# A hybrid attention block on one Trainium2 core: another order for the preparation of the NSA operands, for the modulation strips and for the first stage's weight rounding

## The chip, the core and the metric

The kernel runs on one core of one Trainium2 chip. The metric is device microseconds of a whole launch; lower is better. A core has five engines that run side by side, each through its own list of instructions strictly in order: PE (TensorE, matrix products and transposes; its weight loads are listed apart as PEld), DVE (VectorE), ACT (ScalarE), POOL (GpSimd) and SP (SyncE, which here only issues DMA transfers). An instruction that has to wait for another engine or for a transfer holds up all that stand behind it on its own engine.

## The reference

One transformer block, 512 tokens by 1024 channels, in float32:

```
mod = silu(c) @ ada_w + ada_b                      # six vectors of 1024: sh1, sc1, gt1, sh2, sc2, gt2
h   = rms_norm(x, norm1_gain) * (1 + sc1) + sh1
z   = h @ w_in                                     # 1024 x 4408, cut into latents, q_n, k_c, v_c, k_s, ...
y_mla = mla_attention(latents of z) @ w_o_mla
y_nsa = nsa_attention(q_n, k_c, v_c, k_s, v_s, k_w, v_w, gate logits of z) @ w_o_nsa
x   = x + gt1 * ((sigmoid(g1) * y_mla + sigmoid(g2) * y_nsa) @ w_out)
h2  = rms_norm(x, norm2_gain) * (1 + sc2) + sh2
x   = x + gt2 * ((silu(h2 @ w_gate) * (h2 @ w_up)) @ w_down)
```

In `nsa_attention`, `k_c` and `v_c` (128 columns of z each) are first compressed: overlapping blocks of 32 tokens, plus a position table, go through `silu(flat @ w1) @ w2` with w1 of 2048 x 256. q is normed per head, rotated and used against the compressed, the selected and the windowed keys; the three results are mixed with `sigmoid(gate logits)`.

## The kernel before, in words

Every large product is made in float32 precision from three products of rounded parts. A weight chunk is loaded into a tile `raw`, ACT rounds it into `whi`, DVE subtracts to get the rest `wlo`, and PE adds `hi*whi + hi*wlo + lo*whi` in PSUM. `raw`, `whi` and `wlo` have four buffers each, so that a fourth chunk ahead is the most that can be prepared.

The change lies in the first fifth of the program, up to the start of the NSA attention:

1. `first_gemm` makes `h` and the first 768 columns of `w_in` (query, k_c, v_c) together. For each of eight channel blocks k it needs the modulation column of that block: strips of `ada_w` (tiles `araw`) are multiplied by silu(c) and added up by DVE (`acc`), PE sums them over the partitions (`pm`), DVE makes `modc` from it, PE transposes x (`px`), ACT writes `hTh` (rounded) and `h`, DVE writes `hTl`. PE then runs three groups of eight matmuls per block: A (whi, hTh), B (wlo, hTh) and C (whi, hTl). The instructions of this stage carry a hand-written order per engine (`Paced.strict`). SP issues its transfers in a fixed order too, each waiting for the one eight places earlier.
2. `gemm_wide` for the next 536 columns (`segb2`: k_s, v_s, k_w, v_w, gate logits; tiles `wa`, `wb`), with the preparation of the NSA operands woven in, a step at a time.
3. Three `gemm_tok` passes of 352 columns (`sega`, tiles `ga`; 96 matmuls each), with the rest of the preparation woven in.

The preparation is a chain of generators: `compress_blocks` (transposes of `ZC` to `X2`, position table added in `FF`, rounded and split into `FS`), `compress_w1` (32 matmuls `ph` per K or V, with w1 chunks as weights), `compress_w2` (`hid`, silu, `po`), `compress_out` (norm and rotation of the compressed keys on DVE, `kcr` and `kcd`), `prep_q` (square and sum on ACT and DVE, norm; gain and rotation on POOL; transpose `pq`; split into `QS`), `prep_k` (the same for `UK`, `kd`, `pk`, `KH`, `KL`) and `prep_gates` (exponential on ACT). Beside it `mods()` loads further strips of `ada_w` for the later modulation vectors into the single tile `strip`; DVE multiplies each in two instructions into `macc`, and the next strip can only be issued when both are done.

All calls go through one recording helper, so nearly every instruction carries line 152; rows are told apart by their tiles. After the hand-ordered stage a scheduler places the instructions on each engine; what it made of both programs is shown with the change.

Of the kernel before, what the change touches and what calls it, by code (L numbers as in the profile page):

```python
# [20 lines left out]
P = 128  # L21
S = 512
# [93 lines left out]
def hybrid_block(ctx, tc, a, out):  # L116
# [366 lines left out]
    def first_gemm(w, c0, na, nb, consume_a, consume_b):  # L483
# [57 lines left out]
        products(1, "A")  # L541
        add_rows(acc, s23, 2, (1, 2))
        lo_of(hT[1][1], h, hT[1][0])
        add_rows(acc, s23, 2, range(3, KD))
        products(1, "B")
        scale_x(2 * P, 4 * P, ())
        products(1, "C")
        px = turn_x(2)
        for k in range(2, KD, 2):
            pm = tp.tile([P, S], F32, name="pm", tag="tp")  # L550
            high(k)
            low(k)
            mod_sum(pm, 2, [(acc, ones)], True, True)
            if k > 2:
                products(k - 1, "C")
            more = k + 2 < KD
            if more:
                sn = strips(k + 2, 2)
                load(k + 2)
                load(k + 3)  # L560
            mod_done(pm, k, 2)
            h = modulate(k, px)
            products(k, "A")
            high(k + 1)
            low(k + 1)
            px = turn_x(k + 1)
            lo_of(hT[k][1], h, hT[k][0])
            products(k, "B")
            if more:
                acc = add_rows(None, sn, 2, range(2))  # L570
            h = modulate(k + 1, px)
            if k == 2:
                scale_x(4 * P, D, ())
            products(k, "C")
            if more:
                add_rows(acc, sn, 2, (2, 3))
            lo_of(hT[k + 1][1], h, hT[k + 1][0])
            products(k + 1, "A")
            products(k + 1, "B")
            if more:  # L580
                add_rows(acc, sn, 2, range(4, KD))
                px = turn_x(k + 2)
            else:
                products(k + 1, "C")
        h_last[:] = dve.last, act.last
# [190 lines left out]
        rsqrt(rsf, msf, cpp, f"n{nm}")  # L776
        yield rs

    def prep_q():
        for _ in norm_rows(UQ, 8, "q", rs_n):  # L780
            yield
        for t in range(NT):
            u = UQ[t]
            pool.tensor_tensor(out=u, in0=u, in1=g_n[:, 0:1, :].broadcast_to([P, 8, 64]), op=ALU.mult)
            rope(pool, u[:, :, 0:16], *tables(t, FULL, 8), cpp, f"nq{t}")
            yield
            pq = tp.tile([P, 4, P], F32, name=f"pq{t}", tag="tp")
            for j in range(4):
                pe.transpose(pq[:, j, :], u[:, 2 * j : 2 * j + 2, :].rearrange("p a b -> p (a b)"), ident)
            tcol = slice(t * P, (t + 1) * P)  # L790
            for par in range(2):
                top = slice(64 * par, 64 * par + 64)
                bot = slice(64 * (1 - par), 64 * (1 - par) + 64)
                hi_of(QS[top, par::2, tcol], pq[top, :, :])
                lo_of(QS[bot, par::2, tcol], pq[top, :, :], QS[top, par::2, tcol])
            yield
# [20 lines left out]

    def prep_gates():
        ge = gn.rearrange("p t c -> p (t c)")
        act.activation(out=ge, in_=ge, func=AF.Exp, scale=-1.0)  # L820
        dve.tensor_scalar(out=ge, in0=ge, scalar1=1.0, scalar2=None, op0=ALU.add)
        dve.reciprocal(out=ge, in_=ge)
        gv = gn[:, 0, :].rearrange("p (h b) -> p h b", b=3)
        dve.tensor_scalar(out=gv[:, :, 0], in0=gv[:, :, 0], scalar1=kc_t[:, C_VALID : C_VALID + 1], scalar2=None, op0=ALU.mult)
        yield

    cmp_state = {}

    def compress_blocks(i, nm):
        X2 = cpp.tile([P, 2, 528], F32, name=f"X2_{i}", tag="X2", bufs=1)  # L830
# [22 lines left out]

    def compress_w1(i, nm):
        FS = cmp_state[i]
        ph = sc.tile([P, S], F32, name="ph", tag="sc") if i else mm.tile([P, S], F32, name="ph", tag="mm")
        cmp_state[i] = ph
        w1 = a[f"cmp_w1_{nm}"][0]
        for k0 in range(0, 16, 4):
            h, l = wchunk(rows(w1, k0 * P, 4, 0, 256), 4, 256)  # L860
            for j in range(4):
                pe.matmul(ph[:, :256], FS[:, k0 + j, :], h[:, j, :], start=(k0 + j == 0), stop=False)
                pe.matmul(ph[:, :256], FS[:, k0 + j, :], l[:, j, :], start=False, stop=(k0 + j == 15))
            yield

    def compress_w2(i, nm):
        ph = cmp_state[i]
        hd = cpp.tile([64, 256], F32, name=f"hid{i}", tag="hid", bufs=1)
        act.activation(out=hd, in_=ph[64:128, :256], func=AF.Copy)
        dve.tensor_tensor(out=hd, in0=hd, in1=ph[0:64, :256], op=ALU.add)  # L870
        act.activation(out=hd, in_=hd, func=AF.Silu)
        yield
        pt = tp.tile([P, S], F32, name="pt", tag="tp")
        for j in range(2):
            pe.transpose(pt[:, j * 64 : (j + 1) * 64], hd[:, j * P : (j + 1) * P], ident[:64, :64])
        hidT = cpp.tile([P, 2, 64], F32, name=f"hidT{i}", tag="hidT", bufs=1)
        dve.tensor_copy(out=hidT.rearrange("p a b -> p (a b)"), in_=pt[:, :128])
        w2 = cpp.tile([P, 2, 64], F32, name=f"w2{i}", tag="w2", bufs=1)
        sp.dma_start(out=w2, in_=a[f"cmp_w2_{nm}"][0].rearrange("(j p) d -> p j d", p=P))
        po = tp.tile([P, S], F32, name="po", tag="tp")  # L880
        for j in range(2):
            pe.matmul(po[:64, :64], hidT[:, j, :], w2[:, j, :], start=(j == 0), stop=(j == 1))
        yield
        cmp_state[i] = po
# [85 lines left out]
    def mods():  # L970
# [16 lines left out]
        def finish_row(acc, m, slot, hf):  # L987
            if hf == 0:
                gt[slot] = mcp.tile([P, D], F32, name=f"gt{slot}", tag="gt", bufs=1)
            o = gt[slot][:, hf * S : (hf + 1) * S]  # L990
            sp.dma_start(out=o, in_=a["ada_b"][:, m * D + hf * S : m * D + (hf + 1) * S].broadcast_to([P, S]))
            pm = tp.tile([P, S], F32, name="pm", tag="tp")
            pe.matmul(pm, ones, acc, start=True, stop=True)
            dve.tensor_tensor(out=o, in0=pm, in1=o, op=ALU.add)
# [29 lines left out]
    def need_mod(slot):  # L1024
        while (slot, 1) not in mods_done:
# [2 lines left out]
    mods_gen = mods()  # L1028
    mods_begun = []
    segb2 = gemm_wide(hA, w_in, KD, SEG_B + 768, 280, 256, use_w, use_s, pair_first=True)  # L1030
    pq, pk = prep_q(), prep_k()
    K, V = (0, "k"), (1, "v")
    prep = chain(compress_blocks(*K), part(pq, 5), compress_w1(*K), part(pq, 4), compress_w2(*K), compress_blocks(*V),
                 compress_out(*K), pq, compress_w1(*V), part(pk, 5), compress_w2(*V), pk, compress_out(*V), prep_gates())
    ep_st = scope()
    strip_src["pool"] = ep_st.enter_context(tc.tile_pool(name="ep", bufs=1, reuse_waits="tile"))

    def with_mods(main, every):
        for i, _ in enumerate(main):
            if i % every == 0:  # L1040
                later(mods_gen, 2 if mods_begun else 1)
                mods_begun.append(i)
            yield

    weave(with_mods(segb2, 3), prep, 1, 1)
    sega = chain(*[gemm_tok(hA, w_in, KD, SEG_A + c0, 352, use_a(c0), tag=f"a{c0}") for c0 in (0, 352, 704)])
    weave(with_mods(sega, 6), prep, 2, 1)
    run(prep)
    later(mods_gen, 1)
    ep_st.close()  # L1050
    strip_src.clear()
    cp_st.close()
# [807 lines left out]
```

## Time and profile before

| | |
|---|---|
| median of 3 runs | 875.28 us (873.97 to 875.67) |
| the profiled execution, its own time | 874.82 us |
| its span, from the first to the last instruction | 873.0 us |
| PE busy | 841.4 us (96%), 5052 matmuls |
| DVE busy | 668.7 us (77%) |
| ACT busy | 457.2 us (52%) |
| POOL busy | 119.2 us (14%) |
| mean granted PE clock | 0.989 |

In the rows a time is microseconds from the start of the span: start, duration, engine, operation, tile written <- tiles read, shapes; in square brackets the idle time of the engine just before and what ended it. Matmuls overlap in the pipeline, so their rate is read from start to start and not from the duration. Around the change, the first product stage runs from about 2 to 62 us, `segb2` from 62 to 88, `sega` from 100 to 158, and the attention follows.

### The profile page before, as it was taken

The numbers are of one execution on the slowest core, as the hardware profiler recorded it, in microseconds if no ns is written. First come the engines' busy times: TensorE is split into PE (matmuls) and PEld (weight loads), VectorE is DVE, ScalarE is ACT, GpSimd is POOL, SyncE is SP. The second block draws the span as 40 slices with busy tenths as digits, with TensorE's granted clock in tenths as the row PEclk, the third lists the DMA queues.
The fourth block names the chain that finished last, engine by engine and source line by source line (L and its number), as shares of the span: only waits on it lengthen the run. The fifth ranks groups of instructions, "written<-read, shape, count | busy, mean of one in ns | idle before, by whom it ended". The sixth has DMA issues, their size and how long they took to land.

```text
span 873.0 us, 13961 instructions
## 1 busy us (share of the span) xinstructions
PE 841.4 (96%) x5052; PEld 740.4 (85%) x5052; DVE 668.7 (77%) x1392; ACT 457.2 (52%) x962; POOL 119.2 (14%) x203
## 2 busy tenths in 40 slices
PE   8899799899999999899999999999999999999997
PEld 8789689777777789787788889898999889988996
DVE  5778896668888568688879877975887858965875
ACT  4643655678666567665634255551456326641550
POOL 0002516525342012212200000000000000000000
PEclk9999799999999999999999999999999999999999
DMA  9956646222201123325597753452233313343312
GB/s 309 326 166 189 197 143 170 74 72 74 72 13 61 43 92 98 120 97 180 172 321 253 256 166 118 128 152 90 73 98 121 121 51 113 104 125 92 98 49 97
DMA packets 95706, 115.54 MB, mean 132 GB/s; under 512 B 6565, under 2 KB 68885, under 8 KB 95637
## 3 DMA queue, kind: packets, MB, share of 16 engines
q1 hardware_dynamic: 92596, 108.32, 40.4%
q10 hardware_dynamic: 2400, 4.23, 1.3%
q0 software_dynamic: 640, 2.10, 0.6%
q8 instruction: 40, 0.66, 0.3%
q14 instruction: 30, 0.24, 0.1%
HBM read 106.24 MB, written 8.39 MB: 131 GB/s over the span
## 4 chain that ended last, share of the span: by engine, by line
PE 79%; DVE 8%; DMA 7%; ACT 3%; issue 2%; SPq 1%; ACTq 0%; DVEq 0%
PE d L152 14%; PE fx L152 12%; PE gp L152 9%; PE fy L152 9%; PE pt L152 4%; DMA strip<-in_ada_w_dram 4%; PE av L152 3%; PE ga L152 3%; PE gwo L152 3%; PE gym L152 3%; PE fg L152 3%; PE yn L152 3%; PE wo L152 3%; PE gq L152 2%; PE fu L152 2%
## 5 line engine op out<-in xcount | busy, mean ns | idle before, releaser
L152 ACT ACTIVATE whi<-raw 128x1024 fp32r<-128x1024 f32 (+4 forms) x161 | 141.6, 897 | 133.1 <-PE d L152 51.6
L152 DVE TENSOR_TENSOR wlo<-raw,whi 128x1024 fp32r<-128x1024 f32 (+4 forms) x138 | 149.4, 1090 | 61.3 <-ACT whi L152 60.8
L152 PE MATMUL d<-whi,mh 128*128 128x512 f32 (+1 forms) x180 | 69.9, 391 | 0.6 <-DVE tm L152 0.5
L152 PE MATMUL d<-wlo,mh 128*128 128x512 f32 (+1 forms) x180 | 70.2, 390 | 0.0
L152 PE MATMUL d<-whi,ml 128*128 128x512 f32 (+1 forms) x180 | 67.6, 389 | 0.0
L152 ACT ACTIVATE s<-s,mn 128x384 f32<-128x384 f32 (+2 forms) x96 | 52.5, 548 | 23.1 <-DVE mn L152 22.5
L152 DVE TENSOR_TENSOR plo<-pt,phi 128x512 fp32r<-128x512 f32 (+2 forms) x78 | 46.3, 602 | 19.1 <-ACT phi L152 18.7
L152 PE MATMUL gp<-hTh,whi 128*128 128x512 f32 x128 | 54.4, 425 | 0.0
L152 ACT ACTIVATE phi<-pt 128x512 fp32r<-128x512 f32 (+2 forms) x78 | 39.9, 525 | 27.5 <-PE pt L152 26.9
L152 PE MATMUL gp<-hTh,wlo 128*128 128x512 f32 x128 | 51.2, 400 | 0.0
L152 PE MATMUL gp<-hTl,whi 128*128 128x512 f32 x128 | 50.7, 396 | 0.0
L152 ACT ACTIVATE whi<-s 128x1024 fp32r<-128x1024 f32 (+1 forms) x36 | 30.2, 846 | 32.0 <-PE d L152 18.0
L152 PEld LDWEIGHTS d<-whi,mh 128*128 128x128 f32 x180 | 33.7, 188 | 8.9 <-DVE tm L152 1.2
L152 PE MATMUL fx<-h2h,whi 128*128 128x256 f32 x144 | 41.1, 286 | 0.0
L152 PE MATMUL fx<-h2l,whi 128*128 128x256 f32 x144 | 40.8, 283 | 0.0
L152 PE MATMUL fx<-h2h,wlo 128*128 128x256 f32 x144 | 40.8, 283 | 0.0
L152 PEld LDWEIGHTS d<-whi,ml 128*128 128x128 f32 x180 | 33.8, 188 | 7.7
L152 PEld LDWEIGHTS d<-wlo,mh 128*128 128x128 f32 x180 | 33.8, 188 | 7.4
L152 DVE TENSOR_TENSOR wlo<-s,whi 128x1024 fp32r<-128x1024 f32 (+1 forms) x36 | 33.7, 951 | 7.4 <-ACT whi L152 7.4
L152 PE MATMUL pt<-ident,s 128*128 128x128 f32 x232 | 37.4, 278 | 0.1
L152 POOL TENSOR_TENSOR wlo<-raw,whi 128x512 fp32r<-128x512 f32 x24 | 31.7, 1341 | 23.1 <-ACT whi L152 23.1
L152 PEld LDWEIGHTS pt<-ident,s 128*128 128x128 f32 x232 | 28.1, 142 | 7.6 <-issue 2.1
(432 smaller groups left out, 2666.2 us busy)
## 6 DMA issues: line engine op xcount, KB each, us to landing
raw<-in_ffn_w_gate_dram SPq DMA_DIRECT2D x22, 512.0 KB, 3.9
raw<-in_ffn_w_up_dram SPq DMA_DIRECT2D x22, 512.0 KB, 4.1
raw<-in_ffn_w_down_dram SPq DMA_DIRECT2D x22, 512.0 KB, 3.9
raw<-in_ada_w_dram SPq DMA_DIRECT2D x18, 512.0 KB, 5.0
araw<-in_ada_w_dram SPq DMA_DIRECT2D x32, 256.0 KB, 6.4
raw<-in_w_in_dram SPq DMA_DIRECT2D x16, 512.0 KB, 4.8
strip<-in_ada_w_dram SPq DMA_DIRECT2D x14, 512.0 KB, 5.2
raw<-in_w_in_dram SPq DMA_DIRECT2D x12, 352.0 KB, 3.2
```

Source lines behind the costliest of these rows:

```text
L152: out = call(*args, **kw)
```

## The change

Six edits, all in the order of work; the arithmetic is that of before.

- First stage: ACT rounds two blocks' weights (`high(k)`, `high(k + 1)`) before the modulated x of block k; row 7 of the strips for blocks 2 and 3 goes straight to PE; `pm` and `px` stand ahead of the group C of the block before.
- `prep_q` is cut into `rope_q` (gain, rotation), `turn_q` (transposes) and the norm, which now comes after the compressed keys.
- The preparation chain has another order, with one idle step at its head and three steps per step of `sega` in place of two. The three later query transposes stand apart; `compress_blocks` of V follows `compress_w2` of K.
- `ph` of K takes a buffer of the transposes (`tp`) instead of one of the products (`mm`).
- Strips: 6 generator steps within `segb2` and 10 within the later part of `sega`, in place of 7 and 8 and one at the end. The two loads of `ada_b` rows (`gt`) wait for the first stage's last strip.
- The gate exponential on ACT is held behind the last silu of the compression.

```diff
@@ first_gemm
-        add_rows(acc, s23, 2, range(3, KD))
+        add_rows(acc, s23, 2, range(3, KD - 1))
         products(1, "B")
         scale_x(2 * P, 4 * P, ())
-        products(1, "C")
-        px = turn_x(2)
         for k in range(2, KD, 2):
             pm = tp.tile([P, S], F32, name="pm", tag="tp")
             high(k)
+            high(k + 1)
             low(k)
-            mod_sum(pm, 2, [(acc, ones)], True, True)
-            if k > 2:
-                products(k - 1, "C")
+            if k == 2:
+                mod_sum(pm, 2, [row(s23, 2, KD - 1)], True, False)
+            mod_sum(pm, 2, [(acc, ones)], k > 2, True)
+            px = turn_x(k)
+            products(k - 1, "C")
             more = k + 2 < KD
...
             h = modulate(k, px)
             products(k, "A")
-            high(k + 1)
             low(k + 1)
...
-                px = turn_x(k + 2)
@@ prep_q is cut in two
-    def prep_q():
-        for _ in norm_rows(UQ, 8, "q", rs_n):
-            yield
+    def rope_q():
         for t in range(NT):
...
+    def turn_q():
+        for t in range(NT):
+            u = UQ[t]
             pq = tp.tile([P, 4, P], F32, name=f"pq{t}", tag="tp")
@@ prep_gates, compress_w1, compress_w2, finish_row
+        act.gate = hid_last[0]
         act.activation(out=ge, in_=ge, func=AF.Exp, scale=-1.0)
+        act.gate = None
...
-        ph = sc.tile([P, S], F32, name="ph", tag="sc") if i else mm.tile([P, S], F32, name="ph", tag="mm")
+        ph = sc.tile([P, S], F32, name="ph", tag="sc") if i else tp.tile([P, S], F32, name="ph", tag="tp")
...
+        hid_last[0] = act.last
...
-            sp.dma_start(out=o, in_=a["ada_b"][:, m * D + hf * S : m * D + (hf + 1) * S].broadcast_to([P, S]))
+            late_load(out=o, in_=a["ada_b"][:, m * D + hf * S : m * D + (hf + 1) * S].broadcast_to([P, S]))
@@ the weave
-    prep = chain(compress_blocks(*K), part(pq, 5), compress_w1(*K), part(pq, 4), compress_w2(*K), compress_blocks(*V),
-                 compress_out(*K), pq, compress_w1(*V), part(pk, 5), compress_w2(*V), pk, compress_out(*V), prep_gates())
+    idle = lambda n: iter(range(n))
+    prep = chain(idle(1), compress_blocks(*K), part(rq, 3), mix((rq, 1), (part(tq, 1), 1)), compress_w1(*K),
+                 part(tq, 1), compress_w2(*K), part(tq, 1), compress_blocks(*V), tq, compress_out(*K),
+                 norm_rows(UQ, 8, "q", rs_n), compress_w1(*V), part(pk, 5), compress_w2(*V), pk, compress_out(*V), prep_gates())
...
-    weave(with_mods(segb2, 3), prep, 1, 1)
+    weave(with_mods(segb2, {1: 1, 3: 2, 5: 2, 7: 1}), prep, 1, 1)
-    weave(with_mods(sega, 6), prep, 2, 1)
+    weave(with_mods(sega, {10: 1, 12: 2, 14: 2, 16: 2, 18: 2, 20: 1}), prep, 3, 1)
     run(prep)
-    later(mods_gen, 1)
```

What stands in a row on the engines, at three places. First ACT at the end of the first stage: `hTh_189` is the modulated x of block 6, `hTh_191` that of block 7; `raw 128x768` are weights of this stage, `raw 128x536` those of the next one, whose loads SP issues behind some twenty small ones. Before:

```order
L152 ACTIVATE whi<-raw 128x768
L152 ACTIVATE hTh_189<-px_612,modc 128x512
L152 ACTIVATE h_637<-px_612,modc 128x512
L152 ACTIVATE whi<-raw 128x768
L152 ACTIVATE whi<-raw 128x536 x2
L152 ACTIVATE hTh_191<-px_652,modc 128x512
```

Now:

```order
L152 ACTIVATE whi<-raw 128x768 x2
L152 ACTIVATE whi<-raw 128x536
L152 ACTIVATE hTh_189<-px_626,modc 128x512
L152 ACTIVATE h_642<-px_626,modc 128x512
L152 ACTIVATE whi<-raw 128x536
L152 ACTIVATE hTh_191<-px_655,modc 128x512
```

One rounding of the next stage's weights now stands ahead of block 6's modulated x, where before both stood ahead of block 7's.

Second, PE at the compression of V, in the first third of `sega`. `ZC` are the columns of v_c, `FS` the split blocks made from their transposes, `ga_1204` and `ga_1205` belong to the first pass of `sega` and `ga_1483` to the second. Before:

```order
L152 MATMUL ga_1205<-whi,hTl_192 128x352
L152 MATMUL po<-w_1340,hidT_1338 64x64 x2
L152 MATMUL pt<-ident,ZC_211 128x128
L152 MATMUL pt<-ident,ZC_212 128x128
L152 MATMUL pt<-ident,ZC_213 128x128
L152 MATMUL pt<-ident,ZC_214 128x128
L152 MATMUL ga_1483<-whi,hTh_177 128x352
L152 MATMUL ga_1483<-wlo,hTh_177 128x352
```

Now, to the end of the first pass (`ga_1197`) and on:

```order
L152 MATMUL po<-w_1290,hidT_1288 64x64 x2
L152 MATMUL pq_1295<-ident,UQ_205 128x128 x4
L152 MATMUL ga_1197<-wlo,hTh_191 128x352
L152 MATMUL ga_1197<-whi,hTl_192 128x352
L152 MATMUL pt<-ident,ZC_211 128x128
L152 MATMUL pt<-ident,ZC_212 128x128
L152 MATMUL pt<-ident,ZC_213 128x128
L152 MATMUL pt<-ident,ZC_214 128x128
L152 MATMUL pq_1356<-ident,UQ_206 128x128 x4
L152 MATMUL pt<-ident,kcd 128x64
L152 MATMUL ph<-whi,FS_1345 128x256
```

Before, 48 matmuls of the second pass stood between the transposes of `ZC` and the first `ph` of V; now none does, and all 96 of the second pass come behind the 32 `ph`.

Third, DVE between the end of `segb2` and the start of `sega`, as it stands now (`V` and `gn` empty the product buffers of `segb2`; `wlo 128x704` is the first weight rest of `sega`):

```order
L152 COPY gn<-wa_812 128x24
L152 TENSOR_TENSOR V_2_217<-wb_814,V_2_217 128x2x64
L152 SCALAR_TENSOR_TENSOR macc<-strip,csil,macc 128x512
L152 TENSOR_TENSOR wlo<-raw,whi 128x704
L152 TENSOR_TENSOR QS<-pq_1118,QS 64x4x128
L152 SCALAR_TENSOR_TENSOR macc<-strip,csil,macc 128x512
```

The first rest of `sega` stands behind the first half of the sixth strip; in the order of before it stood behind the sixth strip too, but with all 32 `ph` of K and two query transposes ahead of `sega` on PE, where now 24 and one stand.

More of the change, by code (lines that the diff above doesn't have):

```diff
@@ L827, in hybrid_block @@
     cmp_state = {}
+    hid_last = [None]
     def compress_blocks(i, nm):
@@ L1030, in hybrid_block, with with_mods @@
     segb2 = gemm_wide(hA, w_in, KD, SEG_B + 768, 280, 256, use_w, use_s, pair_first=True)
-    pq, pk = prep_q(), prep_k()
+    rq, tq, pk = rope_q(), turn_q(), prep_k()
     K, V = (0, "k"), (1, "v")
-    prep = chain(compress_blocks(*K), part(pq, 5), compress_w1(*K), part(pq, 4), compress_w2(*K), compress_blocks(*V),
-                 compress_out(*K), pq, compress_w1(*V), part(pk, 5), compress_w2(*V), pk, compress_out(*V), prep_gates())
+    idle = lambda n: iter(range(n))
+    prep = chain(idle(1), compress_blocks(*K), part(rq, 3), mix((rq, 1), (part(tq, 1), 1)), compress_w1(*K),
+                 part(tq, 1), compress_w2(*K), part(tq, 1), compress_blocks(*V), tq, compress_out(*K),
+                 norm_rows(UQ, 8, "q", rs_n), compress_w1(*V), part(pk, 5), compress_w2(*V), pk, compress_out(*V), prep_gates())
     ep_st = scope()
     strip_src["pool"] = ep_st.enter_context(tc.tile_pool(name="ep", bufs=1, reuse_waits="tile"))
-    def with_mods(main, every):
+    def with_mods(main, at):
         for i, _ in enumerate(main):
-            if i % every == 0:
-                later(mods_gen, 2 if mods_begun else 1)
-                mods_begun.append(i)
+            later(mods_gen, at.get(i, 0))
             yield
-    weave(with_mods(segb2, 3), prep, 1, 1)
+    weave(with_mods(segb2, {1: 1, 3: 2, 5: 2, 7: 1}), prep, 1, 1)
     sega = chain(*[gemm_tok(hA, w_in, KD, SEG_A + c0, 352, use_a(c0), tag=f"a{c0}") for c0 in (0, 352, 704)])
-    weave(with_mods(sega, 6), prep, 2, 1)
+    weave(with_mods(sega, {10: 1, 12: 2, 14: 2, 16: 2, 18: 2, 20: 1}), prep, 3, 1)
     run(prep)
-    later(mods_gen, 1)
     ep_st.close()
```

## The prediction

> **What bounds the kernel now.** I read the waits of PE first, since PE is busy for 96% of the span. These are its longest waits in the first 180 us (total, number of times, longest):
>
> ```profile
> PE pq L152 <- POOL UQ L152: 3.2, 1, 3.2
> PE ph L152 <- DVE gn L152: 3.2, 1, 3.2
> PE pm L152 <- DVE acc L152: 2.3, 3, 0.8
> PE pt L152 <- DMA c<-in_c_dram: 2.3, 1, 2.3
> PE ps L152 <- DVE mn L152: 1.8, 1, 1.8
> PE pw L152 <- DVE mn L152: 1.5, 3, 0.6
> PE wa L152 <- ACT hTh L152: 1.4, 1, 1.4
> ```
>
> The two largest stand one behind the other, between `segb2` and `sega`. PE's list in time shows them:
>
> ```profile
> 87.10 0.60 PE L152 MATMUL pq<-ident,UQ 128*128 128x128 f32 x4
> 90.95 1.11 PE L152 MATMUL pq<-ident,UQ 128*128 128x128 f32 x4 [3.24 <-POOL UQ L152]
> 95.28 0.55 PE L152 MATMUL ph<-whi,FS 128*128 128x256 f32 x1 [3.21 <-DVE gn L152]
> ```
>
> The second transposes wait for POOL's rotation, the first `ph` for the copies that empty its product buffer. The gaps cost twice, as the table by windows shows (behind the busy shares of PE, PEld, DVE, ACT and POOL stands the granted clock):
>
> ```profile
> 89.00:90.00 1.00, 0.00 (x0) 0.00 (x0) 0.00 (x0) 0.97 (x6) 0.84 (x4) 0.91 0.96 271
> 100.00:101.00 1.00, 1.00 (x10) 1.00 (x10) 1.00 (x3) 1.00 (x2) 0.00 (x0) 0.97 0.34 123
> 171.00:172.00 1.00, 1.00 (x8) 0.79 (x8) 1.00 (x6) 0.53 (x3) 1.00 (x3) 0.87 0.00 0
> 178.00:179.00 1.00, 1.00 (x4) 0.57 (x5) 0.96 (x3) 0.50 (x2) 0.00 (x0) 0.72 1.09 386
> ```
>
> The clock falls near 89.9 and is full again just after 100; in between it is half. It falls again at 171.9, in the NSA start, and comes back at about 178.3. From 95.28 to 100.05, 4.8 us of PE work ran at half speed, a loss of 2.4 us. So some 9 us of the present time lie at this border, and the change aims work at it. The question is what is late next.
>
> **First stage.** Taking `pm` out of the waits for `acc` (2.3) and `hTh` out of its wait (1.4) would start block 6's group A 3.7 us sooner than now:
>
> ```profile
> 53.07 0.50 PE L152 MATMUL wa<-whi,hTh 128*128 128x512 f32 x1
> ```
>
> ACT's and SP's rows speak against that:
>
> ```profile
> 52.24 0.78 ACT L152 ACTIVATE hTh<-px,modc 128x512 fp32r<-128x512 f32 x1 [6.30 <-DVE modc L152]
> ...
> 55.65 0.65 ACT L152 ACTIVATE whi<-raw 128x536 fp32r<-128x536 f32 x1 [1.22 <-DMA raw<-in_w_in_dram]
> ```
>
> ```profile
> 24.50 1.08 SPq L152 DMA_DIRECT2D gt<-in_ada_b_dram  x2
> ```
>
> One 536-wide rounding now precedes block 6's `hTh` (the ACT rows shown with the change). Its data came at 55.65. Without the two `gt` loads ahead (two 128x512 float32 tiles, 0.52 MB, 1.4 us at the 386 GB/s of the window at 178) I put it at 54.2, within 53.2 to 55.2. Then 0.65 for the rounding and 0.78 for `hTh` give 55.6 for group A, 2.5 us later than now. PE, done with block 5 near 49.5, idles some 6 us, so I charge one half-clock stretch like that at 95, 2.4 us. The stage ends near 62.3 + 2.5 + 2.4 = 67.2. This is not added to the sum yet, since the next border absorbs it.
>
> **From segb2 to sega.** `segb2` runs from here to the first `pq`:
>
> ```profile
> 62.48 0.26 PE L152 MATMUL pt<-ident,vec 50*128 50x50 f32 x1
> ```
>
> That is 24.6 us, so it would end near 91.9. The rotation is by then done, and `ph` has a buffer of its own: both 3.2 us waits go. What is late next is DVE. The rest of `sega`'s first weights stands behind the sixth strip (third place in the change); now it starts here:
>
> ```profile
> 100.63 0.88 DVE L152 TENSOR_TENSOR wlo<-raw,whi 128x704 fp32r<-128x704 f32 x1
> ```
>
> How fast the strips come is in the chain of waits, where they fill nearly all of this stretch; the rates of PE that I use stand there too (start, length, what):
>
> ```profile
> 58.55 5.57 DMA strip<-in_ada_w_dram
> ...
> 86.11 4.40 DMA strip<-in_ada_w_dram
> ...
> 111.63 3.70 DMA strip<-in_ada_w_dram
> ...
> 127.66 2.72 PE ph L152 x24
> ...
> 132.73 6.37 PE ga L152 x40
> ```
>
> DVE's groups from 60 to 135 us give its prices (count, total us, mean ns, then idle before):
>
> ```profile
> L152 DVE TENSOR_TENSOR wlo<-raw,whi 128x1024 fp32r<-128x1024 f32 x8 | 11.5, 1434 | 0.0
> L152 DVE SCALAR_TENSOR_TENSOR macc<-strip,csil,macc 128x512 f32<-128x512 f32 x14 | 10.7, 766 | 5.3 <-DMA strip<-in_ada_w_dram 5.2
> L152 DVE TENSOR_TENSOR wlo<-raw,whi 128x704 fp32r<-128x704 f32 x10 | 9.2, 936 | 0.0
> L152 DVE TENSOR_TENSOR wlo<-raw,whi 128x536 fp32r<-128x536 f32 x6 | 4.4, 731 | 0.0
> L152 DVE TENSOR_TENSOR FF<-X,cols 128x256 f32<-128x256 f32 x8 | 4.4, 586 | 0.1
> L152 DVE TENSOR_TENSOR QS<-pq,QS 64x512 fp32r<-64x512 f32 x5 | 3.3, 684 | 0.1
> L152 DVE COPY X<-pt 64x511 f32<-64x511 f32 x4 | 2.8, 689 | 0.1
> L152 DVE TENSOR_TENSOR FS<-FF,FS 128x512 fp32r<-128x512 f32 x4 | 2.7, 687 | 0.1
> ```
>
> A strip takes 3.7 to 5.6 us to land (I take 4.4, the middle row), two `macc` of 0.77, and about 1.2 of other DVE work between them: 7.1 a cycle. SP's list is 0.7 shorter ahead of the first, so it goes out at 57.8 and the sixth, five cycles on, at 93.4. It lands at 97.8; one `macc` and the rest of 0.88 make `sega`'s first rest ready at 99.5. PE has 24 `ph` (0.113 each, 2.7 us) and one `pq` (0.4) to do from 91.9, with four products that need no rest: done near 96.5. So 3.0 us of idle replace the 6.4 of before. The clock may fall again; from the row at 89 it was falling within 2.4 us of PE's last transposes (87.10 + 0.60). I charge 1.2, bounds 0 and 2.4.
>
> [...]
>
> **Compression of V.** This is the term that decides. Before, 48 products of the second pass cover the chain from `ZC` to `ph`; now PE's order has none there, so PE waits through it. PE's start of this chain before:
>
> ```profile
> 117.47 0.66 PE L152 MATMUL pt<-ident,ZC 128*128 128x128 f32 x4
> ```
>
> After 99.5 the first pass has 92 `ga` at 0.159 (6.37 / 40), 14.6 us, 8 `ph`, 0.9, and four small steps of transposes and `po` near 0.4 each: it ends at 116.6. The `ZC` transposes need a `tp` buffer that DVE's second `QS` frees. Behind the pass DVE has one `zA` copy (estimated 0.5 by its 128x352), `QS` 0.68, `wlo` 1.22 to 1.43, `QS` 0.68 and three tiny ones: 3.4, so 120.0. Then come the norm's tail up to `kcr` and two products on it (1.8), `X` twice (1.4), `FF` twice (1.2), `QS` (0.7), `kcd` (0.6), `FS` (0.7), `QS` (0.7), `FF` twice (1.2), `KL` (0.2), `FS` (0.7): 9.2, with starts between some 9.7, and 129.7. The first 16 `ph` run within it, the last 16 take 1.8: 131.5. Of 15 us PE works 4.6 and idles 10.4.
>
> For comparison: at 132.73 the kernel before had the 32 `ph` done and 148 `ga` (96, 48 and 4); at 131.5 the changed one has 96 `ga` and one `pq` more. The same work stood before at 132.73 − 52 × 0.159 + 0.4 = 124.9. The loss is 131.5 − 124.9 = **+6.6 us**; it already holds the first stage's and the border's gains and losses. Bounds: if the second `QS` comes as soon as its copy (1.2 after the pass), −2.2; if strips and weights pile up on DVE ahead of it, +2. A gap of 10 us brings a half clock for up to 5 us of PE work: +1.5, bounds 0 and 2.5.
>
> **Start of the NSA attention.** The gate exponential, held behind the last silu, shares its table with what follows, so the load at the start of the attention goes:
>
> ```profile
> 162.80 1.28 ACT L152 ACT_TABLE_LOAD   x1
> ```
>
> It lies on the chain, behind it the wait of 1.8 for `mn` in the first view: −1.3. With it the fall of the clock at 171.9 may go: 6.4 us at half, up to 3.2. Together −1.3 to −4.5; I take −2.0, since the waits for `mn` that follow (`pw` 1.5 in three) stay.
>
> [...]
>
> **Sum.** +6.6 + 1.2 + 1.5 − 2.0 = +7.3 on the profiled execution's 874.82, 882.1; the median of the runs shown stands 0.46 above it, so **882.6**. All at their low ends (strips at 3.7: sixth cycle 4.2 sooner, of which PE can use 3.0; `QS` −2.2; clocks −2.7; NSA −2.5) give 872.2; all at their high ends (strips at 5 on average, +3.6; DVE +2; clocks +2.2; NSA +0.7) 891.1. For the likeliest case alone 878.5 to 888.
>
> **Rivals.**
> 1. Faster: the strips do not pace DVE. If each lands in 3.7 (the row at 111.63 did), `sega` begins by 96.5, 3.0 sooner, without loss of clock (−1.2), and DVE comes to V unburdened (−2.2) with the NSA start wholly mended (−2.5): 873.7 less what a shorter gap saves in clock (1.5), 872.2. For it: the 6.4 us of waits are surely gone. Against: five of DVE's waits were for strips (5.2 us in the group row). It decides at `sega`'s first rest: ahead of 96.5 this holds.
> 2. The strips come late or the clock halves in all three gaps: 99.5 moves to 103 (+3.6), clocks +2.2: 888.4. For it: 5.57 at 58.55, while weights load. Against: the median row.
> 3. Gains and losses meet: strips at 3.7, no clock lost in the border, V as forecast, NSA −4.5: 882.6 − 3.0 − 1.2 − 2.5 = 875.9.
> 4. The order doesn't do what it says in the first stage, and group A of block 6 starts at 49.5: this alone changes little, since the strips hold `sega` until 99.5 either way, so it has no chance of its own.
>
> **Chances.** The forecast 0.62, the first rival 0.18, the second 0.11, the third 0.09. About 0.2% (1.75 us) can be told from no change, so 873.5 to 877.0 counts as the same: faster 0.18, same 0.09, slower 0.73. The range is 872.5 to 889: 0.60 of the forecast, the third rival's 0.09, and nearly half of each of the others.
>
> **What would show it.** In the changed profile: ACT waiting for `raw` ahead of block 6's `hTh` and group A near 55.6; no wait of `pq` for POOL; DVE waiting for the sixth strip and the first `wlo` 128x704 ending near 99.5; PE's waits ahead of `ZC`, `kcd` and `ph` of some 10 us together with a half clock behind them; no table load near 163. I am wrong if `sega` starts before 96.5, or if the waits around V are below 5 us: then DVE's chain is shorter than its rows add up to.

## The result: 0.7 to 1.0% slower

| | kernel before | changed kernel |
|---|---|---|
| first comparison, median of 4 runs each | 874.62 us (872.75 to 875.67) | 883.66 us (880.29 to 886.96) |
| ratio, 95% interval | | 1.0105 (1.0063 to 1.0148) |
| second comparison | 874.74 us (17 runs) | 881.29 us (6 runs, 878.92 to 882.90) |
| ratio, 95% interval | | 1.0072 (1.0044 to 1.0099) |
| profiled execution, its span | 873.0 us | 878.5 us |
| mean granted PE clock of the profiled execution | 0.989 | 0.988 |

The forecast was 882.6 us, with 878.5 to 888 for the likeliest case. The ten runs of the changed kernel have a median of 881.9 us; 80 runs of the kernel before, made beside the experiments below on four chips, one of 875.1. That is +6.8 us against a forecast of +7.3.

The waits of PE in the first 180 us of the changed kernel (total, number of times, longest) answer the first view of the prediction:

```profile
PE wa L152 <- ACT hTh L152: 5.0, 1, 5.0
PE pt L152 <- DVE QS L152: 3.6, 1, 3.6
PE pt L152 <- DVE kcd L152: 3.3, 1, 3.3
PE pt L152 <- DMA c<-in_c_dram: 3.2, 1, 3.2
PE ga L152 <- DVE wlo L152: 2.7, 1, 2.7
PE ph L152 <- DVE wlo L152: 2.1, 2, 1.6
PE pw L152 <- DVE mn L152: 1.1, 2, 0.6
PE pm L152 <- DVE acc L152: 0.8, 1, 0.8
PE pq L152 <- DVE kcr L152: 0.8, 1, 0.8
PE ps L152 <- DVE mn L152: 0.2, 1, 0.2
```

The two 3.2 us waits of before (`pq` for POOL, `ph` for `gn`) are gone. In their place PE waits once in the first stage (5.0), at the start of `sega` (2.7 and 2.1) and four times around the compression of V (3.6, 0.8, 3.3 and, below this list, 0.2). `ps` at the start of the attention waits 0.2 in place of 1.8.

The first stage, in ACT's and PE's rows of the changed kernel:

```profile
53.73 0.65 ACT L152 ACTIVATE whi<-raw 128x536 fp32r<-128x536 f32 x1 [9.04 <-DMA raw<-in_w_in_dram]
54.29 0.76 ACT L152 ACTIVATE hTh<-px,modc 128x512 fp32r<-128x512 f32 x1
```

```profile
55.10 0.80 PE L152 MATMUL wa<-whi,hTh 128*128 128x512 f32 x1 [4.99 <-ACT hTh L152]
65.58 0.27 PE L152 MATMUL pt<-ident,vec 50*128 50x50 f32 x1
```

ACT sat idle for 9.0 us until the next stage's weights had landed, with the modulated x of block 6 behind that rounding. The stage ended at 65.58 in place of 62.48.

The start of `sega`, on DVE:

```profile
98.00 0.75 DVE L152 SCALAR_TENSOR_TENSOR macc<-strip,csil,macc 128x512 f32<-128x512 f32 x1 [1.39 <-DMA strip<-in_ada_w_dram]
98.67 0.88 DVE L152 TENSOR_TENSOR wlo<-raw,whi 128x704 fp32r<-128x704 f32 x1
```

The first rest stands behind the sixth strip and is ready at 99.55.

The compression of V, on PE:

```profile
122.46 0.63 PE L152 MATMUL pt<-ident,ZC 128*128 128x128 f32 x4 [3.60 <-DVE QS L152]
123.89 1.09 PE L152 MATMUL pq<-ident,UQ 128*128 128x128 f32 x4 [0.80 <-DVE kcr L152]
128.27 0.34 PE L152 MATMUL pt<-ident,kcd 64*128 64x64 f32 x1 [3.30 <-DVE kcd L152]
128.78 0.58 PE L152 MATMUL ph<-whi,FS 128*128 128x256 f32 x1 [0.17 <-DVE FS L152]
```

and in the chain that ended last (start, length, what), where the 32 `ph` take 6.1 us; at 0.113 each they would be 3.6 us of work:

```profile
128.78 6.12 PE ph L152 x32
134.89 6.38 PE ga L152 x40
```

The last 16 of the 32 need the second `FS`, which DVE finished at 131.96. At 0.113 each they would have ended near 133.8, so the half clock costs some 1.1 us at this place and not the whole difference of 2.5.

The granted clock stands behind the busy shares of the five engines in the windows of 1 us; these are the edges of the half-clock stretches in the changed kernel (the first of them begins at 55.0):

```profile
58.00:59.00 1.00, 1.00 (x8) 0.96 (x7) 0.00 (x0) 0.25 (x1) 0.00 (x0) 0.80 0.83 163
99.00:100.00 1.00, 0.39 (x1) 0.39 (x2) 0.97 (x2) 0.00 (x0) 0.00 (x0) 0.68 0.03 10
102.00:103.00 1.00, 1.00 (x6) 1.00 (x5) 1.00 (x3) 0.00 (x0) 0.00 (x0) 0.62 0.72 108
123.00:124.00 1.00, 0.20 (x2) 0.14 (x2) 0.86 (x6) 0.80 (x2) 0.00 (x0) 0.62 0.82 280
133.00:134.00 1.00, 1.00 (x8) 1.00 (x8) 1.00 (x2) 0.40 (x2) 0.00 (x0) 0.76 0.08 6
```

So the clock is half from 55.0 to 58.4, 99.4 to 102.8 and 123.2 to 133.5, and not at the start of the attention, where it was half from 171.7 to 178.6 before (by the rows of 0.87 and 0.72 in the prediction).

**Where the time went.** At 134.9 the changed kernel has done the work that stood at 124.9 before (the prediction's count: 96 `ga`, 32 `ph`, all query transposes): 10.0 us behind. Later in the attention, at the first `gk`, it is 4.9 behind (311.08 and 306.15). So some 5 us came back at the start of the attention: 1.6 by the shorter wait of `ps`, and 3.4 by the 6.8 us of half clock that are not there. At the end it is 5.5 behind in span; in between, the changed kernel's profile has one more stretch of half clock, 3.4 us from 362.2, that the other one lacks.

### The profile page after: what moved, and what is told of

Its sections match the earlier page's. It is cut to its first block, busy times and chain, and to the rows that moved or that the text cites. A ratio compares the mean times of both kernels' runs of the same rounds, so it can differ in the third digit from the quotient of the medians.

```text
span 878.5 us, 13987 instructions
## 1 busy us (share of the span) xinstructions
PE 842.3 (96%) x5060; PEld 742.5 (85%) x5060; DVE 673.5 (77%) x1391; ACT 455.4 (52%) x960; POOL 112.6 (13%) x203
## 4 chain that ended last, share of the span: by engine, by line
PE 80%; DVE 8%; DMA 6%; issue 3%; ACT 2%; SPq 1%; POOL 0%; ACTq 0%; DVEq 0%; POOLq 0%
PE d L152 14%; PE fx L152 12%; PE gp L152 9%; PE fy L152 9%; PE ga L152 5%; PE pt L152 4%; PE av L152 3%; PE gwo L152 3%; PE gym L152 3%; PE fg L152 3%; PE wo L152 2%; PE gq L152 2%; PE fu L152 2%; DMA strip<-in_ada_w_dram 2%; PE ps L152 2%
## 5 line engine op out<-in xcount | busy, mean ns | idle before, releaser
L152 PE MATMUL ga<-wlo,hTh 128*128 128x352 f32 x96 | 32.4, 337 | 2.7 <-DVE wlo L152 2.7
```

Source lines behind the costliest of these rows:

```text
L152: out = call(*args, **kw)
```

## The experiments

All times are medians, compared with the kernel before on the same chip; the ratio has its 95% interval.

| run | what differs | us | ratio to before |
|---|---|---|---|
| changed kernel, again | nothing | 881.29 | 1.0072 (1.0044 to 1.0099) |
| v_covered | changed, V's chain covered | 875.24 | 0.9994 (0.9970 to 1.0018) |
| before_three_steps | before, V's chain uncovered | 878.19 | 1.0039 (1.0016 to 1.0063) |
| no_hold | changed, exponential not held | 881.94 | 1.0068 (1.0044 to 1.0091) |
| before_hold | before, exponential held | 871.55 | 0.9943 (0.9915 to 0.9970) |
| hth_first | changed, block 6's x first | 878.98 | 1.0062 (1.0040 to 1.0084) |
| three_strips | changed, fewer strips ahead of `sega` | 902.12 | 1.0308 (1.0278 to 1.0338) |
| all_three | changed, three mends | 886.19 | 1.0134 (1.0105 to 1.0164) |
| clock_kept | changed, PE kept busy ahead of `kcd` | 884.62 | 1.0126 (1.0098 to 1.0153) |
| mend_two | changed, two mends | 875.18 | 1.0013 (0.9991 to 1.0036) |
| mend_three_early | changed, three mends, strips earlier | 871.92 | 0.9972 (0.9943 to 1.0001) |
| hold_first_stage | before, hold and first stage | 869.03 | 0.9923 (0.9901 to 0.9945) |

The changed kernel itself, run again:

> The changed kernel itself, on one chip with the three next ones, so that they are compared with it and not with its first four runs only. Expected 881 to 884; its profile may lose more or fewer stretches of 3.4 us to the half clock than the first one, and if the time follows their number, the spread of the kernel (880.3 to 887.0) is that.

It came out at 881.29, within the expectation. Its second profile (span 880.6) has the same waits around V (3.6, 3.3, 0.8). Up to 136 us it lost six stretches of 3.4 us to the half clock in place of five; up to 870 us both profiles have six, so the 2.1 us between these two executions are not explained by their number.

### V's chain covered, and uncovered

```diff
-                 part(tq, 1), compress_w2(*K), part(tq, 1), compress_blocks(*V), tq, compress_out(*K),
-                 norm_rows(UQ, 8, "q", rs_n), compress_w1(*V), part(pk, 5), compress_w2(*V), pk, compress_out(*V), prep_gates())
+                 part(tq, 1), compress_w2(*K), compress_blocks(*V), compress_out(*K), part(tq, 1), idle(5), tq,
+                 norm_rows(UQ, 8, "q", rs_n), idle(5), compress_w1(*V), part(pk, 5), compress_w2(*V), pk, compress_out(*V), prep_gates())
```

> The changed kernel with one difference: five and five idle steps in the preparation chain and the two later query transposes behind compress_out of K, so that 48 products of sega's second pass stand between the ZC transposes and the first ph of V again, as before the change. Theory A (the uncovered chain of V is the loss): PE's waits ahead of ZC, pq, kcd and ph of V (3.6, 0.8, 3.3 and 2.1 us in the changed kernel's profile) shrink below 1.5 us together, the clock stays full from 105 to 160 us, and the time falls by 9 to 11 us, from 883.7 to 873 to 875. Rival B (PE only waits there for work that the first stage and the strips made late): the waits move to other products of sega, and the time stays above 880.

PE in that run, the first of the `ZC` transposes and the first `ph` of V:

```profile
117.57 0.66 PE L152 MATMUL pt<-ident,ZC 128*128 128x128 f32 x4
125.71 0.28 PE L152 MATMUL ph<-whi,FS 128*128 128x256 f32 x1
```

Neither row has a wait in brackets, and the clock stays full there (1.00 from 104 to 171). The time is 875.24, 6.7 us below the ten runs of the changed kernel, just above the 873 to 875 that Theory A expected and well below the 880 of Rival B. So the order of the preparation, through the missing cover, is what made the change a loss. The gain is smaller than the 10 us between the two profiles at V; in that run's profile a 2.5 us wait of `pk` for `kd` and the half clock at the start of the attention stand again.

The mirror of it, in the kernel before:

```diff
-    weave(with_mods(sega, 6), prep, 2, 1)
+    weave(with_mods(sega, 6), prep, 3, 1)
```

> The kernel before with one number changed: three steps of the preparation chain per step of sega in place of two, so that only 8 products of the first pass stand between the ZC transposes and the first ph of V, and none of the second; everything else as before. Theory A: PE waits some 6 to 9 us around V with a half clock behind it, and the time rises by 6 to 10 us to 881 to 885. Rival B (the loss comes from the first stage and the border): no change within 2 us of 874.6.

```profile
115.31 0.66 PE L152 MATMUL pt<-ident,ZC 128*128 128x128 f32 x4
123.79 0.58 PE L152 MATMUL ph<-whi,FS 128*128 128x256 f32 x1 [6.56 <-DVE rq_m_kc L152]
```

The wait is there as expected (6.6 us, with the clock at half from 121.5 to 128.3), and the time rises, by 3.4 us in the ratio (1.4 to 5.5) and not by 6 to 10. What the expectation left out is the other side of the same edit: the preparation ends sooner, and the wait of `ps` at the start of the attention falls from 1.8 to 0.2, though the clock falls there as it did before (half from 176.1 to 182.9). Uncovering V costs more than it brings, but it does bring something.

### The hold of the gate exponential

```diff
@@ no_hold: the changed kernel without
-        act.gate = hid_last[0]
         act.activation(out=ge, in_=ge, func=AF.Exp, scale=-1.0)
-        act.gate = None
@@ before_hold: the kernel before with
+        act.gate = hid_last[0]
         act.activation(out=ge, in_=ge, func=AF.Exp, scale=-1.0)
+        act.gate = None
```

> The changed kernel without the hold of the gate exponential. The prediction's term for the hold was -2.0 us within -1.3 to -4.5; in the profiles the distance from the end of sega to the steady part of the attention shrank by 5. Theory A: a table load of 1.28 us stands at the NSA start again, PE's wait ps <- mn is near 1.8 and the clock falls to half for 6 us: 3 to 5 us slower than the changed kernel, 887 to 889. Rival C (the start of the attention mended itself because the preparation was done earlier): the clock stays full there and the time within 1.5 us of 883.7.

> The kernel before with the hold of the gate exponential alone. Theory A: the table load near 163 us goes, the half clock at 172 to 178 with it, and the time falls by 3 to 5 us to 870 to 872. Smaller size, as predicted: -2.0, 872.6. Rival C: no change, 874.6.

In the kernel before, the hold alone gives 871.55, 0.3 to 0.85% faster: Theory A's size, but only half of its mechanism shows. In that run's profile the load at 162.8 is gone and `ps` waits 0.4 in place of 1.8:

```profile
164.62 0.33 PE L152 MATMUL ps<-KH,QS 128*128 128x128 f32 x1 [0.36 <-DVE mn L152]
```

The half clock behind it is not gone. It lasts from 170.5 to 180.7, 10.2 us in place of 6.8. This execution took 876.36, the slowest of the eight, so where the gain beyond the 1.4 us of that wait comes from is not shown.

In the changed kernel, taking the hold out costs nothing that can be told (881.94 against 881.9): Rival C. ACT's and PE's rows of the run without the hold show why:

```profile
173.28 1.28 ACT L152 ACT_TABLE_LOAD   x1
```

```profile
176.79 0.33 PE L152 MATMUL ps<-KH,QS 128*128 128x128 f32 x1 [0.21 <-DVE mn L152]
```

The table load is back, but PE has 15 `gp` products from 172.3 to 176.0 to do meanwhile, and waits 0.2 us. Before, the last of 15 `gp` began at 162.88, while the load ran from 162.80, and PE waited 1.8 for `ps`. So in the changed kernel the hold is not what mended the start of the attention. That the earlier preparation did is the likely reading: in before_three_steps, which has it without the hold, `ps` waits 0.2 too. The two edits mend the same wait, and their gains don't add.

### The first stage

```diff
+        more_hi = lambda k: k + 2 < KD
...
             high(k)
-            high(k + 1)
+            if more_hi(k):
+                high(k + 1)
             low(k)
...
             products(k, "A")
+            if not more_hi(k):
+                high(k + 1)
             low(k + 1)
```

> The changed kernel, but in the last pair of blocks the second rounding stays where it was before, by which ACT makes block 6's modulated x ahead of the first 536-wide rounding, and DVE makes sega's first rest behind five strips in place of five and a half. Theory A (prediction): PE's wait wa <- hTh (5.0) falls to about 1 and the half clock at 55 to 58 goes, the first stage ends some 4 us sooner; of that sega keeps only what DVE gives it: its first rest is ready one half strip cycle earlier, near 95 to 96, a gain of 3 to 4 us, 879 to 880. Rival D (the strips don't hold sega): sega starts right behind segb2's last product and the ph, near 90, a gain of 8 or more. Rival E (all is held by the strips): less than 1 us.

PE's rows at the end of the first stage and at the start of `sega`:

```profile
60.26 0.26 PE L152 MATMUL pt<-ident,vec 50*128 50x50 f32 x1
94.58 0.66 PE L152 MATMUL ga<-wlo,hTh 128*128 128x352 f32 x1 [0.23 <-DVE wlo L152]
```

The wait for `hTh` fell to 1.0, the stage ended at 60.3, and `sega`'s first product with a rest came at 94.58 in place of 99.61 (101.7 in the second profile): 5 to 7 us sooner, more than the half cycle of Theory A. Of that V's chain took back half. PE reached it sooner and waited longer:

```profile
119.04 1.09 PE L152 MATMUL pt<-ident,ZC 128*128 128x128 f32 x4 [4.56 <-DVE QS L152]
123.33 0.34 PE L152 MATMUL pt<-ident,kcd 64*128 64x64 f32 x1 [2.15 <-DVE kcd L152]
126.64 0.58 PE L152 MATMUL ph<-whi,FS 128*128 128x256 f32 x1 [2.98 <-DVE FS L152]
```

9.7 us of waits in place of 7.9, with four stretches of half clock (13.7 us in all). The total, 878.98, is what Theory A named, but by another way.

Whether the strips hold back what the first stage gains was put to the test once more, in the kernel before with the hold, where six whole strips stand ahead of `sega`'s first rest and V is covered. The first stage is that of hth_first:

> The kernel before with two parts of the change: the hold of the gate exponential (871.6 alone) and the first stage of the run hth_first (pm and px ahead of the group C of the block before, second rounding early except in the last pair, the gt loads behind the last strip). Strips, preparation and V's cover as before, six strips ahead of sega's first rest. Theory A (prediction: what the first stage gains is held back by the strips): the first stage ends near 60.3 in place of 62.5, but sega's first product with a rest stays within 1 us of 101.2, the waits of pq and ph grow by what was gained, and the time stays within 1 us of 871.6. Rival D (it passes through): sega's first rest comes 2.2 us sooner, 869.4.

PE's end of the first stage, and DVE's first rest:

```profile
60.54 0.26 PE L152 MATMUL pt<-ident,vec 50*128 50x50 f32 x1
```

```profile
97.28 0.88 DVE L152 TENSOR_TENSOR wlo<-raw,whi 128x704 fp32r<-128x704 f32 x1
```

The first stage ends 1.9 us sooner, and `sega`'s first rest starts 3.3 us sooner than before (100.63). Rival D holds in the rows: the gain passes through. The strips are no fixed clock. The first of them is issued at 56.61 in place of 58.55 and the sixth at 87.57 in place of 94.15, so that they follow each other every 6.2 us in place of 7.1; why they do is not shown. The time of 869.03, 6.3 us below the kernel before (0.9923, 0.9901 to 0.9945), beats both kernels. What the first stage adds to the hold (871.55 alone) is 1.8 us by the ratios and 2.5 by the medians; the two intervals overlap, so its size is not settled.

### Fewer strips ahead of sega

```diff
-                    sp.dma_start(out=raw.rearrange("p (r n) -> p r n", r=2), in_=rows(ada, r0 * P, 2, m * D + hf * S, S))
+                    d = sp.dma_start(out=raw.rearrange("p (r n) -> p r n", r=2), in_=rows(ada, r0 * P, 2, m * D + hf * S, S))
+                    if "pool" in strip_src:
+                        follow_dma(d.ins, pe.last)
```

> The changed kernel with the strips of this stretch ordered behind PE's last product at the point of the program where each is asked for: three of them stand ahead of sega's first rest instead of five and a half, the others come behind the V compression. Theory A: DVE's waits for strips before sega fall from 7 us to about 3, PE's wait ga <- wlo (2.7) and the half clock behind it go, sega starts near 96 in place of 99.6, and since V's chain stays uncovered the gain is these 3 to 5 us, 879. Rival D: no change, as DVE has the copies of segb2 to do in any case.

At the border the expectation held: `sega`'s first product with a rest at 97.16, with a wait of 0.5 us. The time did not: 902.12. PE at the start of the attention, and DVE ahead of it:

```profile
184.26 0.47 PE L152 MATMUL pw<-KH,QS 128*128 128x160 f32 x1 [14.42 <-DVE mn L152]
```

```profile
181.95 1.54 DVE L152 SCALAR_TENSOR_TENSOR macc<-strip,csil,macc 128x512 f32<-128x512 f32 x2 [3.99 <-DMA strip<-in_ada_w_dram]
```

The last four strips that were put off came one after the other between 158 and 182, each with its transfer ahead of it on a single buffer, and DVE's `mn`, for which the attention waits, stood behind them. I had looked at what leaves the border and not at where it goes.

All three mends (hth_first, V covered as in v_covered, three strips) had the same fate:

> The changed kernel with the three mends together: block 6's modulated x ahead of the next stage's rounding, three strips ahead of sega, and V's chain covered by 48 or more products. Theory A: first stage 4 us shorter, sega starts near 91 to 92 in place of 99.6, no wait above 1.5 us around V: 883 - 7.5 - 9 = 866.5, within 864 to 870, below the kernel before. Rival B: the gains cancel against each other, not below 872.

It did the first 192 products of `sega` by 130.1 us (151.3 in the changed kernel, 140.2 before), 10.1 us ahead of the kernel before, and lost more than that behind them:

```profile
150.96 1.11 PE L152 MATMUL pk<-ident,kd 128*128 128x128 f32 x4 [4.45 <-DVE kd L152]
159.68 0.66 PE L152 MATMUL pk<-ident,kd 128*128 128x128 f32 x4 [2.20 <-DVE kd L152]
...
171.19 0.50 PE L152 MATMUL pw<-KH,QS 128*128 128x160 f32 x1 [8.18 <-DVE mn L152]
```

The strips stand ahead of the wait for `mn`, as in three_strips. I took the ten idle steps that gave V its cover for the cause of the late keys (`kd`). Two runs therefore filled the cover with preparation that is needed anyway:

```diff
+                 part(tq, 1), compress_w2(*K), compress_blocks(*V), compress_out(*K), part(tq, 1), tq,
+                 norm_rows(UQ, 8, "q", rs_n), part(pk, 5), compress_w1(*V), compress_w2(*V), pk, compress_out(*V), prep_gates())
@@ mend_three_early, with the strips ordered as in three_strips
-    weave(with_mods(sega, {10: 1, 12: 2, 14: 2, 16: 2, 18: 2, 20: 1}), prep, 3, 1)
+    weave(with_mods(sega, {2: 1, 4: 2, 6: 2, 8: 2, 10: 2, 12: 1}), prep, 3, 1)
```

> The changed kernel with block 6's modulated x ahead of the next stage's rounding, and the preparation chain in another order with no idle step: compress_out of K, the query norm and half of the norm of the selected and windowed keys stand between compress_blocks and compress_w1 of V, which puts 24 products of sega's second pass into V's chain; the two later query transposes come behind. The strips stay as the scheduler puts them (five ahead of sega's first rest). Theory A: sega starts near 94.6, PE waits about 9.7 - 3.8 - 1 = 5 us in V's chain and not for QS, the preparation ends ahead of the NSA start: 881.3 - 2.3 - 6 = 873 (871 to 876). Rival B (what is mended here comes back as a wait at the start of the attention, as in the run with all three mends): pk waits for kd or pw for mn above 3 us, and the time is above 877.

> As the run before it, with three strips ahead of sega, the other five asked for eight steps of sega earlier than in the run with all three mends (886.2). Theory A: what that run lost was the strips and keys that came late at the NSA start (waits pw <- mn 9.5, pk <- kd 6.6); with both earlier the waits shrink below 3 us together, and the 7 to 9 us that it was ahead at the end of the second pass of sega are kept: 866 to 870. Rival: the DVE work only shifts, a wait of 5 us or more stands at the NSA start again, and the time stays above 874.

mend_two gave 875.18, level with the kernel before, at the upper end of Theory A's range; its longest wait behind the first stage's border is `pk` for `kd`, 2.9 us in two. mend_three_early gave 871.92 (0.9943 to 1.0001), better than all_three by 14 us, but not the 866 to 870 expected, and not told apart from the kernel before: one wait stayed.

```profile
PE pk L152 <- DVE kd L152: 4.9, 3, 2.8
```

Since `pk` waits for `kd` in both runs, without any idle step, these steps were at most a part of why the keys came late (6.6 us in all_three).

### The clock alone

```diff
             lo_of(QS[bot, par::2, tcol], pq[top, :, :], QS[top, par::2, tcol])
+            if t == 3:
+                hot3 = sc.tile([P, S], F32, name="hot3", tag="sc")
+                pe.gate = pe.last
+                keep_clock(hot3, 28)
+                pe.gate = None
```

> The changed kernel with 28 products of a constant tile (128x256, results unused) on PE between the last query transposes and the transposes of kcd, in the place where PE waited 3.3 us; nothing else moves. The wait stays, the clock alone is tested. Theory A (the waits around V cost twice, by the wait and by the half clock behind it): the half clock behind 126 us ends one or two stretches of 3.4 us sooner, the 32 ph take 3.6 to 4.8 us in place of 6.1, and the time falls by 1.5 to 2.5 us, 879 to 880. Rival: the clock falls in any case (it is set by the first wait alone), and the time is the changed kernel's, 881 to 884.

```profile
126.16 4.53 PE L152 MATMUL hot<-heat 128*128 128x256 f32 x28
130.62 0.27 PE L152 MATMUL pt<-ident,kcd 64*128 64x64 f32 x1
```

Locally it did what it was to do: the half clock ended at 128.3, 4.3 us behind the `ZC` transposes in place of 11, and the `ph` ran at 0.113. But the 28 products outlasted the wait by 0.8 us, and the last 16 `ph` then waited 0.7 for the second `FS`, which DVE finished 9.5 us behind `ZC` as in the changed kernel. The last `ph` began 11.4 us behind `ZC` in place of 12.2: 0.7 us won. DVE's chain leaves no more to win there, whatever the clock. The time shows nothing of it (884.62), and this run's profile has the half clock at the start of the attention that the changed kernel's lacked. The size named by Theory A is not confirmed. Why the median of these six runs lies above the changed kernel's stays open.

## Why the prediction was right

**First stage.** Right in mechanism and place. The data for the first 536-wide rounding came at 53.73 (54.2 in the prediction), group A of block 6 started at 55.10 (55.6), and PE waited 5.0 (6). The half clock lasted 3.4 us and not 4.8, so that the stage ended at 65.58 and not 67.2.

**From segb2 to sega.** The term was sized by the strip cycle, and its result fits to 0.1 us: the sixth strip was issued at 93.84 (93.4), the first rest was ready at 99.55 (99.5). The half clock behind the gap of 2.7 us (3.0) came, 3.4 us long, for 1.7 (1.2 charged). Two shorter waits stood just ahead, which I had not foreseen (2.1 us of `ph` for `wlo`), and whether the gap would have been enough without them was not tried. Two agreements here are luck. In the second profile of the same kernel the first rest was ready at 101.7, 2 us later. And that PE was done at 96.96, near the 96.5 of the prediction, comes of two errors: PE reached the first `pq` at 90.02 and not at 91.9, and then lost those 2.1 us. The prediction's own terms (91.9, 2.7, 0.4 and four products of 0.16) add to 95.6, so by them the gap was 3.9 and not 3.0, and the lowest time would be 871.3 and not 872.2.

**Compression of V.** Right, and shown by v_covered. Waits of 7.9 us stand in PE's rows (some 10 in the prediction); the second `QS` held `ZC` for 3.6 us (3.4), and from `ZC` to the second `FS` it took 9.5 us (9.7, by the DVE rows of before). The half clock behind these waits lasted 10.2 us, but it cost only some 1.1 of the 1.5 charged, because the last 16 `ph` would have waited for the second `FS` in any case; clock_kept, where the clock was full again, won 0.7. With the border, the kernel was 10.0 us behind, where 9.3 were forecast: the border's clock was 0.5 dearer, the first pass of `sega` about 0.5 longer beside that, and V's clock 0.4 cheaper; 0.1 and 0.2 at `sega`'s start and at `ZC` and −0.2 in the chain make up the rest.

**Start of the attention.** The effect was right and its cause wrong. The table load is gone (ACT's only load between 60 and 180 us, 1.28 long, stands at 137.81 ahead of the gate exponential, and the exponentials of the attention follow from 169.40 without another) and PE's wait with it, but no_hold shows that the load would have been hidden. "So the load goes" holds as a reason only in the kernel before, where the hold alone brought 0.3 to 0.85%. In the changed kernel something else mended the wait, most likely the earlier preparation, which the prediction did not count. In size, -2.0 was charged within -1.3 to -4.5; between the profiles about 5 came back, of which 3.4 are the half clock. Its absence is luck in part: hth_first and clock_kept, which have the hold and the early preparation too, have a half clock of 3.4 us there.

**Rivals.** The fourth one was dismissed by the words that the strips hold `sega` until 99.5 either way. hold_first_stage refutes that: its first rest came 3.3 us sooner with six strips ahead. The step that failed took the strips' cycle of 7.1 us as given, while it shrank to 6.2 in that run. For the changed kernel this did no harm, since the error lies in what a faster first stage would be worth. The first rival (the strips don't pace DVE) fell by its own test: `sega`'s first rest was not ahead of 96.5. Of the second, the half clock in all three gaps came true, but the first rest came at 99.55 and not near 103 (101.7 in the second profile). Of the third, a gain of 4.5 or more at the attention came, the quicker strips and the full clock at the border did not.

The sum (+7.3) fits the medians (+6.8) better than its parts do: the V side was 0.7 too low, the attention's gain 3 too small, and 0.6 was lost behind it, so that the two profiles are only 5.5 apart. That the medians lie nearer to the forecast than the profiles do is luck; the granted clock ran from 0.980 to 0.990 over the ten runs and from 0.980 to 0.995 over the 80, while the two profiles have 0.988 and 0.989.

## What to carry to other kernels

- When steps of a side chain are put in another order, count what is left between a producer and its consumer on the busiest engine: here 48 products of 0.16 us, 7.6 us in all, covered most of a chain of 9.5 us, and a finer interleaving left none.
- Work that is put off has to be followed to where it lands. The strips moved away from one border came back as waits of 8 and 14 us at the next stage's start.
- A part worth taking may sit in a change that loses: the hold and the first stage, with one rounding left in its old place, gave 869.03 us where the whole change gave 881.9.

## What the hardware showed that was not expected

**The half clock came in pieces of 3.4 us.** The stretches in the first 200 us of the two first profiles are 10.2 and 6.8 us before, 3.4, 3.4 and 10.2 after, so 3, 2, 1, 1 and 3 pieces. Their starts lie whole pieces apart too: 89.8 and 171.7 by 24, and 55.0, 99.4 and 123.2 by 13 and 7. The same gaps did not always cost a piece. The start of the attention has the same PE busy time in a window of 4 us in both kernels, and the clock fell behind it in the one and not in the other:

```profile
168.00:172.00 4.00, 2.87 (x20) 2.37 (x19) 3.79 (x23) 3.09 (x14) 1.09 (x3) 0.97 0.00 0
172.00:176.00 4.00, 4.00 (x13) 2.92 (x12) 3.04 (x11) 3.80 (x10) 3.00 (x4) 0.50 0.00 0
```

before, and the same slice of the program after, at the end of its window still with a full clock:

```profile
176.00:180.00 4.00, 2.87 (x20) 2.39 (x19) 3.79 (x23) 3.09 (x14) 1.09 (x3) 1.00 0.00 0
```

Counted on in such pieces from the starts of the half clock, the slice is cut at different points. Before, the piece from 168.33 to 171.75 had PE busy for 2.29 us, 67% of it, and the clock was half behind it. In the changed kernel the pieces from 174.44 and from 177.86 had 2.85 and 2.84, 83%, and it stayed full. The gap at the start of `sega` lies in one piece, from 95.95 to 99.36, with PE busy for 1.01 us, 30%, and the clock was half behind it. Whether the busy share of a piece decides was not tested.

The clock goes with most of the spread of the runs as well. Over the 80 runs of the kernel before (870.5 to 881.3 us) the time follows the mean granted clock with a correlation of -0.90: 13 runs at 0.980 to 0.984 have a median of 879.5, 23 runs at 0.991 to 0.995 one of 872.7. So one profile's half-clock stretches are a sample, and an edit that removes gaps may pay partly by making them rarer: hold_first_stage has 0.991 to 0.994 in its six runs and spreads over 3.4 us.

**Three rows of DVE took longer beside POOL.** The rotation that starts earlier in the changed kernel lies beside DVE's work of the first stage's end. An instruction of DVE of the same form, in the kernel before and then in the changed one, with POOL's row of the latter:

```profile
66.85 0.28 DVE L152 SCALAR_TENSOR_TENSOR trig<-trig 128x120 f32<-128x120 f32 x1
```

```profile
66.50 1.39 DVE L152 SCALAR_TENSOR_TENSOR trig<-trig 128x120 f32<-128x120 f32 x1
```

```profile
65.21 5.53 POOL L152 TENSOR_TENSOR UQ<-UQ,g_n 128x512 f32<-128x512 f32 x4 [28.15 <-DVE trig L152]
```

1.39 in place of 0.28 us is about one POOL instruction of that row (5.53 / 4); the rounding rest beside it took 1.73 in place of 0.71. DVE's row at 70.81, just behind POOL's last instruction of that row, has its old time again (0.74). A second `trig` row of that form, at 69.53, took 1.36. Not every instruction beside POOL was longer: four copies of `ZC` from 65.05 took 1.41 together, where two took 0.75 before. Why is not shown. The prediction had counted the moved rotation only as PE's wait that it removes.
